# Memory projection with the weights' rest last in a step, and attention outputs split behind the attention's latest VectorE operation

## The chip, the cores and the metric

The kernel runs on one core of one Trainium2 chip. The metric is the device time of one execution in microseconds (us). Three runs of the kernel before the change gave 2080.78, 2082.31 and 2084.13 us; their median, 2082.31 us, is the time before. A separate, profiled execution gives the trace; its times are counted from the first instruction.

Engines are named as the profile names them: PE is TensorE (PEld its weight loads), DVE is VectorE, ACT is ScalarE, POOL is GpSimd, SP is SyncE.

## The reference, cut to what matters

The program is an encoder of two layers over 512 tokens of width 1024, with 256 memory tokens. Each layer is a gated feed-forward block, a self-attention mixer, a cross attention to the memory, and a second feed-forward block. The change touches the end of the mixer's stage: the projection of the memory tokens to keys and values (`m @ wkv`), and the projection of the attention's outputs (`@ w_out`).

```python
for layer in range(DEPTH):
    h = h + 0.5 * swiglu(rmsnorm(h, g), wg, wu, wd)
    if layer % 2 == 0:
        h = h + even_mixer(rmsnorm(h, mix_g), *mix_params, t5_bias, layer)
    else:
        h = h + odd_mixer(rmsnorm(h, mix_g), *mix_params)
    h = h + memory_xattn(rmsnorm(h, mg), rmsnorm(mem, sg), wq, wkv, qg, kg, wo)
    h = h + 0.5 * swiglu(rmsnorm(h, g), wg, wu, wd)

def memory_xattn(h, m, wq, wkv, qg, kg, wo):
    ...
    k, v = jnp.split(m @ wkv, 2, axis=-1)
    ...

# the end of both mixers (attention outputs o of 1024 features):
    return jnp.concatenate([out_a, out_b], axis=-1) @ w_out     # even
    return chunk_band_attention(q, k, v, rel_bias) @ w_out      # odd
```

## The kernel before, in words

**Products in three parts.** Each large operand is split into a leading part (suffix h, written by ACT in the type fp32r) and a rest (suffix l, written by DVE or POOL as the difference). A product of two such operands is three matmuls: lead by lead, lead by rest, rest by lead. Weights come through `wload` (line 166): a DMA into `wf`, then `wh` on ACT (line 161) and `wl` on DVE or, for a share of the loads, on POOL (line 163).

**Who sets the order.** PE executes its instructions in the order in which the program writes them down. The other engines' orders are made by a scheduler that simulates the program: what stands earlier in the program, or in a `high_priority` block, goes first among what is ready in that simulation. `issue_after(ins)`, used through `behind` (line 153), adds an edge of order without a semaphore: every instruction traced in its block on the engine of `ins` comes behind `ins` in that engine's queue. It does nothing to instructions on other engines.

**The weave.** In a mixer, `weave` (line 82) interleaves two generators: `gemm`, which yields an estimated cost after each piece of products, and `att`, which yields a gap. For each gap, pieces are pulled until their costs have used it up; what goes beyond is not carried over. In layer 0 a pair of heads (`attend64`, line 851) goes through these steps: queries and keys are transposed (lines 766 and 785), gap `A_QK` = 3900; the previous pair's second head is finished (transposes of the probabilities, line 837, gap `A_PT` = 1950; products with the values, line 864, gap `A_PV` = 0); the logits of head 0 (line 812), gap `A_S` = 600; the logits of head 1, gap 600; head 0 is finished (1950 and 0). In layer 1 the gaps are 4550 (`C_QK`), 2600 (`C_PT`), 600 (`C_PV`), 600 (`C_S`).

**`mark`.** `self.mark` is the latest DVE instruction that the attention has traced: the rest of the queries (line 776, the second of two), the last of four reductions of a softmax (line 825), or the last of the three rests of transposed probabilities (line 841).

**Order of the stage.** In `gemm` the six chunks of the mixer's input projection (line 706) come first, then `mem_kv` (line 1087), then `mix_out` (line 1318), which calls `out_proj` (line 635). `mem_kv` goes through 8 blocks k of the memory's width. A block has 12 matmuls of 128x512 into four PSUM banks (tag pa): for two halves i of the memory tokens and two halves c of the output, `mh` by `wh`, `mh` by `wl`, `ml` by `wh`. It yields 1300 after each i. Then the banks are copied out (lines 1110 to 1117). `out_proj` takes one attention output k after the other: at the start of a step `parts(k)` splits the output `os[k]` into `oh` (ACT, line 1327) and `ol` (DVE, line 1329) where that is not done yet, and the step's 12 matmuls (line 657) read oh, ol, oh for each of four banks, with a yield of 1300 after each second bank. The first half of the output takes k = 0 to 3, the second k = 0 to 6; what is left comes when the attention is over.

## Time and profile before

| | |
|---|---|
| median of three runs | 2082.31 us |
| the profiled execution's own time | 2083.2 us |
| its span, first to last instruction | 2081.4 us |
| granted TensorE clock, mean over the span | 0.999 |
| POOL busy | 362.0 us, 17% |
| DVE busy | 1563.2 us, 75% |
| ACT busy | 1136.0 us, 55% |
| first and last start of a matmul of `mem_kv` (line 1104) | 556.8 and 1612.8 us |
| first start of a matmul of `out_proj` that reads an `oh` | 598.4 us |

The span lies within the profiled execution's own time; 1.8 us lie around it. A row of a timeline gives the start, the duration, the engine, the line of the kernel, the operation, the tile written and the tiles read, and, in brackets, how long the engine was idle before it and who ended that. PE rows overlap, since matmuls are pipelined: the distance of two starts is what a matmul costs, not the duration in its row.

### The profile page before, as it was taken

The page shows a single profiled execution, that of the slowest core. Times are in us where ns is not written, and L with a number is a line of the kernel's source. Part 1 is how long each engine was busy: PE and PEld are TensorE (multiplying, and loading weights), DVE is VectorE, ACT ScalarE, POOL GpSimd, SP SyncE. Part 2 cuts the span into 40 slices and gives each one's busy share as a digit, 9 for nine tenths or more (in the row PEclk, how much of TensorE's full clock was granted, in tenths as well). Part 3 has the DMA queues.
Part 4 walks back from the last instruction along what each step waited for, and adds up shares of the span by engine and source line. Part 5 has one row for each costly group of instructions (what it writes and reads, how often), then busy time and mean ns, then how long its engine had stood idle before and what let it go on. Part 6 is the DMA issues. An engine that isn't in the chain of part 4 may idle for free.

```text
span 2081.4 us, 32525 instructions
## 1 busy us (share of the span) xinstructions
PE 2049.1 (98%) x12834; PEld 1826.4 (88%) x12834; DVE 1563.2 (75%) x2246; ACT 1136.0 (55%) x1701; POOL 362.0 (17%) x319
## 2 busy tenths in 40 slices
PE   8999999999999999999999999999999999999999
PEld 7989897888788889898989899988888888989897
DVE  8858687699676697685889677685668688958676
ACT  6636354556686565362556354444778566626442
POOL 1101003345431120000020000013453122000000
PEclk9999999999999999999999999999999999999999
DMA  7837535222241166574356466344224224737633
GB/s 234 208 115 196 151 95 173 88 87 81 83 136 61 61 194 171 143 190 123 107 167 180 124 178 177 100 127 148 91 81 130 94 71 144 193 120 189 166 99 94
DMA packets 86121, 279.65 MB, mean 134 GB/s; under 512 B 9680, under 2 KB 12880, under 8 KB 85968
## 3 DMA queue, kind: packets, MB, share of 16 engines
q1 hardware_dynamic: 74448, 235.62, 34.5%
q0 software_dynamic: 11520, 41.95, 11.7%
q8 instruction: 101, 1.65, 0.3%
q14 instruction: 52, 0.43, 0.1%
HBM read 271.24 MB, written 6.29 MB: 133 GB/s over the span
## 4 chain that ended last, share of the span: by engine, by line
PE 87%; DVE 7%; ACT 3%; issue 2%; DMA 1%; POOL 1%; SPq 0%; ACTq 0%; DVEq 0%; POOLq 0%
PE ps_pa L468 24%; PE ps_pa L706 11%; PE ps_pa L604 10%; PE ps_pb L468 10%; PE ps_pb L604 10%; PE ps_pa L657 4%; PE ps_pa L323 3%; PE ps_pb L812 2%; PE ps_pa L1254 1%; PE ps_pb L864 1%; PE ps_pa L1104 1%; PE ps_pb L837 1%; PE ps_pb L657 1%; PE ps_pa L1023 1%; PE ps_pb L323 1%
## 5 line engine op out<-in xcount | busy, mean ns | idle before, releaser
L161 ACT ACTIVATE wh<-wf 128x1024 fp32r<-128x1024 f32 (+2 forms) x211 | 215.4, 1022 | 334.7 <-PE ps_pa L604 114.6
L163 DVE TENSOR_TENSOR wl<-wf,wh 128x1024 fp32r<-128x1024 f32 (+2 forms) x169 | 199.5, 1184 | 32.5 <-ACT wh L161 30.5
L447 DVE TENSOR_TENSOR wl<-s,wh 128x1024 fp32r<-128x1024 f32 x108 | 132.0, 1222 | 47.3 <-ACT wh L446 47.3
L446 ACT ACTIVATE wh<-s 128x1024 fp32r<-128x1024 f32 x108 | 114.6, 1061 | 94.5 <-PE ps_pb L468 33.6
L446 ACT ACTIVATE wh<-wf 128x1024 fp32r<-128x1024 f32 x84 | 89.1, 1061 | 97.4 <-PE ps_pa L468 34.4
L525 POOL DMA_DIRECT2D s<-l_ffn_wq x40 | 35.5, 887 | 519.4 <-ACT s L524 486.4
L163 POOL TENSOR_TENSOR wl<-wf,wh 128x1024 fp32r<-128x1024 f32 x42 | 101.4, 2415 | 137.7 <-ACT wh L161 135.8
L706 PE MATMUL ps_pa<-wh,xh 128*128 128x512 f32 x384 | 122.5, 400 | 0.0
L706 PE MATMUL ps_pa<-wh,xl 128*128 128x512 f32 x384 | 119.7, 393 | 0.0
L706 PE MATMUL ps_pa<-wl,xh 128*128 128x512 f32 x384 | 119.1, 391 | 0.0
L498 POOL DMA_DIRECT2D s<-l_ffn_wq x40 | 35.6, 890 | 444.5 <-DMA s<-l_ffn_wq 150.2
L447 DVE TENSOR_TENSOR wl<-wf,wh 128x1024 fp32r<-128x1024 f32 x84 | 102.6, 1222 | 6.8 <-ACT wh L446 3.8
L614 DVE TENSOR_TENSOR dn<-ps_pa,R 128x512 f32<-128x512 f32 x48 | 33.1, 689 | 85.3 <-PE ps_pa L604 84.9
L604 PE MATMUL ps_pb<-hh,wh 128*128 128x512 f32 x352 | 95.5, 389 | 0.0
L604 PE MATMUL ps_pb<-hl,wh 128*128 128x512 f32 x352 | 95.4, 389 | 0.0
L604 PE MATMUL ps_pb<-hh,wl 128*128 128x512 f32 x352 | 95.4, 389 | 0.0
L228 POOL TENSOR_TENSOR acc<-acc,sq 128x512 f32<-128x512 f32 (+1 forms) x37 | 52.3, 1415 | 246.5 <-ACT sq L227 245.4
L604 PE MATMUL ps_pa<-hh,wh 128*128 128x512 f32 x328 | 88.9, 390 | 0.0
L604 PE MATMUL ps_pa<-hh,wl 128*128 128x512 f32 x328 | 88.6, 389 | 0.0
L604 PE MATMUL ps_pa<-hl,wh 128*128 128x512 f32 x328 | 88.6, 389 | 0.0
L614 DVE TENSOR_TENSOR dn<-ps_pb,R 128x512 f32<-128x512 f32 x48 | 33.0, 688 | 71.2 <-PE ps_pb L604 70.8
L706 PEld LDWEIGHTS ps_pa<-wh,xl 128*128 128x128 f32 x384 | 72.5, 189 | 15.9
(377 smaller groups left out, 5892.3 us busy)
## 6 DMA issues: line engine op xcount, KB each, us to landing
wf<-l_ffn_wq SPq DMA_DIRECT2D x120, 512.0 KB, 3.9
s<-l_ffn_wq SPq DMA_DIRECT2D x80, 512.0 KB, 4.9
s<-l_ffn_wq POOLq DMA_DIRECT2D x80, 512.0 KB, 6.4
wf<-l_ffn_wd SPq DMA_DIRECT2D x64, 512.0 KB, 4.2
wf<-l_w_in SPq DMA_DIRECT2D x48, 512.0 KB, 3.3
wf<-l_ffn_wd SPq DMA_DIRECT2D x32, 384.0 KB, 3.2
wf<-l_mem_wkv SPq DMA_DIRECT2D x16, 512.0 KB, 3.3
wf<-l_w_out SPq DMA_DIRECT2D x16, 512.0 KB, 3.3
```

The costliest lines, as they stand in the source:

```text
L161: self.leading = nc.scalar.activation(wh[:, sl], w[:, sl], AF.Copy)
L163: eng.tensor_sub(wl[:, sl], w[:, sl], wh.bitcast(F32)[:, sl])
L228: self.summed = (eng or nc.gpsimd).tensor_add(acc[:, :n], acc[:, :n], sq[:, :n])
L323: nc.tensor.matmul(p, w[a][:, k * P:(k + 1) * P], xs[k][c], start=k == order[0] and a == c == 0, stop=k == order[-1] and a == 1)
L446: self.leading = nc.scalar.activation(h, t, AF.Copy)
L447: self.parted = nc.vector.tensor_sub(l, t, h.bitcast(F32))
L468: self.nc.tensor.matmul(bank[:, sl], w[a][:, o:o + P], xs[k][b], start=first and z == a == b == k == 0, stop=z == a == 1 and k == KB // 2 - 1,
L604: self.nc.tensor.matmul(bank, w[a][:, j * P:(j + 1) * P], h, start=j == a == e == 0, stop=j == nb - 1 and (a, e) == ops[-1])
L614: nc.vector.tensor_mul(t, bank, f.R)
L657: nc.tensor.matmul(banks[dd], a[:, o:o + P], parts(k)[b], start=k == first and a is wh and b == 0, stop=k == last and a is wl)
L706: nc.tensor.matmul(banks[i], xs[k][a][:, i * P:(i + 1) * P], w[b][:, kk * 512:kk * 512 + 512], start=k == a == b == 0, stop=k == KB - 1 an ...
L812: nc.tensor.matmul(bank[:, o:o + n], a, b[:, :n], start=c == 0, stop=c == len(ops) - 1)
```

## The change

In `mem_kv` the matmuls of a block are regrouped: first, for each half i of the memory tokens, the four that read `wh` (`mh` by `wh` and `ml` by `wh`, two halves c), with a yield of 900 after each i; then the four that read `wl`, with a yield of 800. The number of matmuls and the sum of the yields of a block (2600) stay the same; a block is now pulled in three pieces of 4 matmuls and not in two of 6.

In `mix_out` the split of an attention output is traced in a block behind `self.mark`. Of the two instructions only the rest `ol` is on DVE, the engine of `mark`, so only it gets the edge.

```diff
@@ mem_kv
+            def products(i, ops):
+                for c in range(2):
+                    for a, b in ops:
+                        nc.tensor.matmul(banks[c][i], a[:, i * P:(i + 1) * P], b[:, c * 512:(c + 1) * 512],
+                                         start=k == 0 and a is mh and b is wh, stop=k == KB - 1 and b is wl)
+
             for i in range(2):
-                for c in range(2):
-                    for n, (a, b) in enumerate(((mh, wh), (mh, wl), (ml, wh))):
-                        nc.tensor.matmul(banks[c][i], a[:, i * P:(i + 1) * P], b[:, c * 512:(c + 1) * 512],
-                                         start=(k == 0 and n == 0), stop=(k == KB - 1 and n == 2))
-                yield 1300
+                products(i, ((mh, wh), (ml, wh)))
+                yield 900
+            for i in range(2):
+                products(i, ((mh, wl),))
+            yield 800
@@ mix_out, parts(k)
-                oh = self.xp.tile([P, S], F32R, name="oh", tag="xs", bufs=2 * KB)
-                nc.scalar.copy(oh, o)
-                ol = self.xp.tile([P, S], F32R, name="ol", tag="xs", bufs=2 * KB)
-                nc.vector.tensor_sub(ol, o, oh.bitcast(F32))
+                with self.behind(self.mark):
+                    oh = self.xp.tile([P, S], F32R, name="oh", tag="xs", bufs=2 * KB)
+                    nc.scalar.copy(oh, o)
+                    ol = self.xp.tile([P, S], F32R, name="ol", tag="xs", bufs=2 * KB)
+                    nc.vector.tensor_sub(ol, o, oh.bitcast(F32))
```

## The prediction

> **What bounds the kernel now.** The page comes first: PE is busy for almost the whole span.

> ```profile
> span 2081.4 us, 32525 instructions
> PE 2049.1 (98%) x12834; PEld 1826.4 (88%) x12834; DVE 1563.2 (75%) x2246; ACT 1136.0 (55%) x1701; POOL 362.0 (17%) x319
> ```

> So PE sets the end, and only 2081.4 - 2049.1 = 32.3 us of the span are not PE work. An edit helps by removing such idle time, or a slower clock, and harms by adding it. Next I read the waits of PE (who waited for whom: us in total, times, longest) for what the edits touch, and the four places in PE's timeline.

> ```profile
> PE ps_pb L837 <- DVE qz L776: 2.5, 2, 2.0
> PE ps_pa L1104 <- POOL wl L163: 1.9, 2, 1.0
> PE ps_pa L1104 <- DVE wl L163: 0.5, 1, 0.5
> 543.86 0.52 PE L837 MATMUL ps_pb<-ident,e 128*128 128x128 f32 x3 [2.05 <-DVE qz L776]
> 561.05 0.50 PE L1104 MATMUL ps_pa<-wl,mh 128*128 128x512 f32 x1 [1.02 <-POOL wl L163]
> 581.67 0.50 PE L1104 MATMUL ps_pa<-wl,mh 128*128 128x512 f32 x1 [0.91 <-POOL wl L163]
> 1604.78 0.50 PE L1104 MATMUL ps_pa<-wl,mh 128*128 128x512 f32 x1 [0.55 <-DVE wl L163]
> ```

> The memory's projection waits three times for a `wl`, and the transposes at 543.86 wait 2.05 us for a PSUM bank that a `qz` on DVE has to free. Why that `qz` was late stands in the timelines of DVE and POOL:

> ```profile
> 540.82 2.17 DVE L1329 TENSOR_TENSOR ol<-x,oh 128x512 fp32r<-128x512 f32 x1
> 543.02 0.69 DVE L776 TENSOR_TENSOR qz<-ps_pb,qz 64x512 fp32r<-64x512 f32 x1
> 540.07 2.37 POOL L163 TENSOR_TENSOR wl<-wf,wh 128x1024 fp32r<-128x1024 f32 x1 [1.27 <-ACT wh L161]
> L1329 DVE TENSOR_TENSOR ol<-x,oh x16: 677/690/2489, 530.4 to 1659.9; 128x512 fp32r<-128x512 f32 x16
> ```

> An attention output's rest `ol`, not needed by PE before the matmuls of line 657 much later, stood in DVE's queue ahead of the `qz`, and took 2.17 us beside a POOL split where the median of its line is 690 ns. That idle time had a second price. The stretches around it (us, then PE, PEld, DVE, ACT, POOL, and the granted clock):

> ```profile
> 541.20:544.60 3.40, 1.35 (x11) 1.10 (x10) 3.31 (x4) 2.26 (x5) 1.24 (x1) 1.00 0.30 92
> 544.60:548.00 3.40, 3.40 (x10) 2.62 (x9) 1.55 (x3) 0.29 (x1) 0.00 (x0) 0.50 0.17 67
> 548.00:551.40 3.40, 3.40 (x19) 3.00 (x19) 1.23 (x1) 1.73 (x3) 0.00 (x0) 1.00 0.00 0
> 556.00:598.00 42.00, 40.08 (x223) 32.91 (x222) 31.38 (x73) 34.15 (x73) 21.90 (x21) 1.00 0.42 138
> ```

> After a stretch in which PE worked 1.35 of 3.40 us, the granted clock was 0.50 for one stretch as long: 10 matmuls instead of 19, worth 3.40 x 0.5 = 1.7 us. The last row holds the waits of 1.02 and 0.91 us, and its clock is 1.00.

> **Part one, the memory's projection.** 8 x 12 matmuls per layer stay, and so do their DMAs, `wh` and `wl`. In a block the first reader of `wl` moves from the second place to the ninth, so `wl` has seven matmuls more, and often a step of the attention besides. The spacing of matmuls is in these rows of PE:

> ```profile
> 598.42 0.48 PE L657 MATMUL ps_pa<-oh,wh 128*128 128x512 f32 x1
> 598.74 0.39 PE L657 MATMUL ps_pa<-ol,wh 128*128 128x512 f32 x1
> 598.97 0.40 PE L657 MATMUL ps_pa<-oh,wl 128*128 128x512 f32 x1
> ```

> 0.23 us each (0.32 after another kind of work), so seven are 1.6 us, more than the longest of the three waits. All three go: 1.02 + 0.91 + 0.55 = 2.48 us. `ml` is needed one place, 0.23 us, earlier; in no row does PE wait for it, and I take nothing. The pieces are smaller: behind each logits step of a softmax come 4 matmuls, not 6, so the transposes of head 0 come 2 x 2 x 0.23 = 0.9 us sooner after their logits. The tightest place of the stage has PE's transposes at 569.15 and the end of the last exponential's sum on ACT at 567.90 + 0.19 = 568.09, a margin of 1.06 us:

> ```profile
> 569.15 1.26 PE L837 MATMUL ps_pb<-ident,e 128*128 128x128 f32 x10
> 567.90 0.19 ACT L826 ACTIVATION_READ_ACCUMULATOR e<-e,m 128x1 f32 x1
> ```

> That covers it; without that cover it would cost some tenths. All four banks of the projection now end within its last four matmuls, so their evictions come in one bunch just ahead of the first output step; this lies beside a longer wait there, below.

> **Part two, the split behind the mark.** The `ol` at 540.82 leaves its place, so the 2.05 us and the 1.7 us of half clock go: 3.75 us. With 2.48, the gains are 6.2 us.

> Against that: `parts(k)` is called at the start of step k, the mark is then the newest DVE operation of the attention, and the second matmul of the step reads `ol`. Before, `ol` could be done long ahead. Now the way from the attention's matmuls over ACT and DVE to the mark, and then `ol`, lies between PE's last attention work and this matmul, with only the pieces in between as cover. What is queued behind the waiting `ol` on DVE waits with it; what waits for it is PE, and everything behind PE.

> Where each step falls follows from the weave's costs. Layer 0: the 24 pieces of the projection start in the last gap (3000) of the diff attention and take 4; then per pair of heads gaps of 600, 600, 1950, 3900, 1950 take 1, 1, 3, 5, 3 pieces. 22 are used up when the second group's queries and keys are transposed; its gap of 3900 takes the last two (900 + 800) and two output pieces (1300 each). So k=0 starts 8 matmuls behind a `qz` mark. Then k=1 starts directly behind the transposes of a finish (gap 1950, two pieces), k=2 directly behind the logits of head 0, k=3 directly behind the next transposes, k=4 and k=5 each one piece (6 matmuls) behind transposes; k=6 and 7 come later than their mark. Layer 1, counted the same way (gaps 4550, 2600, 600, 600, 600): k=0 is 4 matmuls behind transposes, k=2 six behind a `qz`, k=4 six behind transposes; k=1, 3, 5 share their predecessor's mark and are clear.

> How late a mark is, measured from the start of the first matmul that follows its PE work, shows in the rows of PE and DVE of the trace of before. Behind transposes (typical, latest, earliest):

> ```profile
> 615.88 0.48 PE L657 MATMUL ps_pa<-oh,wh 128*128 128x512 f32 x1
> 617.79 0.55 DVE L841 TENSOR_TENSOR pz2l<-ps_pb,pz2h 128x384 fp32r<-128x384 f32 x1
> 580.28 0.48 PE L1104 MATMUL ps_pa<-wh,mh 128*128 128x512 f32 x1
> 584.42 0.55 DVE L841 TENSOR_TENSOR pz2l<-ps_pb,pz2h 128x384 fp32r<-128x384 f32 x1
> 1651.76 0.48 PE L657 MATMUL ps_pa<-oh,wh 128*128 128x512 f32 x1
> 1653.07 0.55 DVE L841 TENSOR_TENSOR pz2l<-ps_pb,pz2h 128x384 fp32r<-128x384 f32 x1
> ```

> The mark ends 618.34 - 615.88 = 2.46 us after that point, at the latest 4.69, at the earliest 1.86. I take 2.46, the middle. Behind logits, with an `ol` that already happens to follow its mark:

> ```profile
> 610.11 0.58 PE L657 MATMUL ps_pa<-oh,wh 128*128 128x512 f32 x1
> 610.53 0.40 PE L657 MATMUL ps_pa<-ol,wh 128*128 128x512 f32 x1
> 611.11 0.69 DVE L825 CUSTOM_DVE_ANT_0 e<-ps_pb,bias 128x512 f32<-128x512 f32 x1
> 611.72 0.69 DVE L1329 TENSOR_TENSOR ol<-x,oh 128x512 fp32r<-128x512 f32 x1
> ```

> The mark ends after 611.80 - 610.11 = 1.69 us, and `ol` 0.61 us behind it, at 2.30. Behind queries and keys (layer 0 twice, layer 1):

> ```profile
> 575.08 0.48 PE L1104 MATMUL ps_pa<-wh,mh 128*128 128x512 f32 x1
> 578.15 0.69 DVE L776 TENSOR_TENSOR qz<-ps_pb,qz 64x512 fp32r<-64x512 f32 x1
> 602.64 0.69 DVE L776 TENSOR_TENSOR qz<-ps_pb,qz 64x512 fp32r<-64x512 f32 x1
> 1626.33 0.48 PE L657 MATMUL ps_pa<-oh,wh 128*128 128x512 f32 x1
> 1628.84 0.69 DVE L776 TENSOR_TENSOR qz<-ps_pb,qz 64x512 fp32r<-64x512 f32 x1
> ```

> That is 3.76 and (against 598.42, quoted above) 4.91 us in layer 0, 3.20 in layer 1. The 4.91 had the projection's evictions in front of it; the new order has them behind the `qz`, so I take 3.76 and 3.20.

> The wait of PE is mark + 0.61 - cover, where the cover is 0.32 (0.42 behind logits) plus 0.23 per matmul in between. Layer 0: k=0 3.76 + 0.61 - 2.16 = 2.2; k=1 and k=3 2.46 + 0.61 - 0.32 = 2.75 each; k=2 1.9; k=4 and k=5 2.46 + 0.61 - 1.70 = 1.4 each: 12.4 us. Layer 1: k=0 2.46 + 0.61 - 1.24 = 1.8; k=2 3.20 + 0.61 - 1.70 = 2.1; k=4 1.4: 5.3 us. Together 17.7 us. With the earliest marks (1.86, 3.20) it is 13.5 us, with the latest (4.69, 4.91) 34 us; 17.7 is nearer to the low end because the latest rows had foreign DVE work ahead of the mark. An `ol` that meets a POOL split can take up to 2.49 us (the line's longest), 1.8 more than I count; the high end holds one or two of these.

> Then the clock. Four of these waits (k=0, 1, 3 of layer 0, k=2 of layer 1) are 2.05 us or longer, the length that halved the clock at 544.60, where 1.02 us at 561.05 did not. Whether a wait falls into one such stretch or is cut in two is not known, so I count two of four: 2 x 1.7 = 3.4 us.

> [...]

> Sum: -6.2 + 17.7 + 3.4 = +14.9 us on the profiled execution's 2083.2 (its span of 2081.4 and 1.8 around it): 2098.1. The median of the runs is 0.9 lower, so 2097.2 us.

> **The rivals.**
> 1. The waits come, but the clock stays up: +11.5 us, 2093.8. For it speaks that a wait cut in two by the boundary of such stretches may be as harmless as the 1.02 us were; against it that the one wait of 2.05 us did lower the clock. [...]
> 2. Faster: the marks come early enough. With the output splits gone from the stretch ahead, DVE and ACT have less queued, and if the marks then end so early that all covers suffice, only the gains stay: 2082.3 - 6.2 = 2076.1. It decides, for k=1 and k=3, at a mark that ends 0.3 us ahead of the first matmul behind the transposes; the earliest row has it 1.86 us behind, so nearly everything speaks against it, but for a step that begins elsewhere than I counted.
> 3. Only the steps directly behind their mark wait (k=1, 2, 3 of layer 0, 7.4 us) and the others are covered, without a change of the clock: 2082.3 - 6.2 + 7.4 = 2083.5.
> 4. The edge does nothing to DVE's order; the `ol` stays early, and the three `wl` waits alone go: 2082.3 - 2.5 = 2079.8.

> **How the numbers follow.** Within 0.2%, 4.2 us either way, is about what a measurement of this kernel can tell from no change. Forecast 0.47 (2097.2), rival 1 0.33 (2093.8), rival 2 0.09 (2076.1), rival 3 0.08 (2083.5), rival 4 0.03 (2079.8). Slower: 0.47 + 0.33 = 0.80; same: 0.08 + 0.03 = 0.11; faster: 0.09. The first two reach from 13.5 us of waits without a slower clock (+7.3, 2089.6) up to waits halfway between 17.7 and 34 (25.8) with three slow stretches (5.1): +24.7, 2107.0. The range goes down to 2083 to take in rival 3.

> **What would show it.** Right: PE waits in the matmuls of line 657 for `ol` of the split's line, six times between about 595 and 640 us and three times in layer 1, 1.4 to 2.8 us each; `ol` directly behind a mark in DVE's rows; no wait for `wl` in the memory's projection, none of 2 us for `qz` at 543; half clock right behind one or more of the new waits. Wrong: `ol` still ahead of 560 us, or matmuls that read it without idle time ahead of them.

## The result and the profile after

| | before | after |
|---|---|---|
| median of five runs | 2082.31 us (2080.22 to 2086.06) | 2113.43 us (2110.08 to 2117.51) |
| the profiled execution's own time | 2083.2 us | 2111.0 us |
| its span | 2081.4 us | 2109.2 us |
| granted TensorE clock | 0.999 | 0.996 |

The time after is 1.0147 times the time before (95% interval 1.0128 to 1.0167): 31.1 us slower, where 14.9 us were forecast. The sign was right and the waits that were named came, but the size was twice the forecast and lies above the range, and one of the two parts was taken for a gain and is a cost. The trace read below is of the second fastest of the five executions, so only 27.8 of the 31.1 us are in it; the mean granted clock of the other four was 0.992 to 0.995.

The page of after:

```profile
PE 2059.1 (98%) x12830; PEld 1829.8 (87%) x12834; DVE 1562.0 (74%) x2246; ACT 1136.6 (54%) x1701; POOL 361.9 (17%) x319
```

DVE, ACT and POOL do what they did. PE's busy time is 10 us longer with the same matmuls, part of which is a slower clock, below; the rest of the 27.8 us is waiting. The waits of PE in after (in total, times, longest), first for 340 to 740 us (layer 0), below the dots for 1400 to 1760 us (layer 1):

```profile
PE ps_pa L657 <- DVE ol L1336: 9.7, 6, 2.4
PE ps_pb L937 <- POOL orr L248: 2.4, 1, 2.4
PE ps_pa L657 <- ACT qk L1116: 1.4, 1, 1.4
PE ps_pa L657 <- DVE x L670: 1.2, 1, 1.2
...
PE ps_pa L657 <- ACT qk L1116: 2.8, 1, 2.8
PE ps_pa L657 <- DVE ol L1336: 2.8, 2, 2.1
PE ps_pa L1104 <- ACT qk L731: 1.4, 1, 1.4
PE ps_pb L812 <- DVE x L869: 1.0, 1, 1.0
```

The three waits for `wl` in the memory's projection are gone, and so is the 2.0 us wait for `qz`. In their place stand the forecast waits for `ol`, 9.7 + 2.8 = 12.5 us, and some that were not forecast: for the copies of the projection's banks (L1116), for `orr`, for `x`, for `qk` of L731. The `ol` waits one by one, in PE's timeline of after:

```profile
600.37 0.80 PE L657 MATMUL ps_pa<-ol,wh 128*128 128x512 f32 x1 [2.01 <-DVE ol L1336]
608.20 0.50 PE L657 MATMUL ps_pa<-ol,wh 128*128 128x512 f32 x1 [2.39 <-DVE ol L1336]
616.84 0.79 PE L657 MATMUL ps_pa<-ol,wh 128*128 128x512 f32 x1 [1.77 <-DVE ol L1336]
626.39 0.50 PE L657 MATMUL ps_pa<-ol,wh 128*128 128x512 f32 x1 [2.04 <-DVE ol L1336]
653.98 0.50 PE L657 MATMUL ps_pa<-ol,wh 128*128 128x512 f32 x1 [0.66 <-DVE ol L1336]
660.27 0.50 PE L657 MATMUL ps_pa<-ol,wh 128*128 128x512 f32 x1 [0.87 <-DVE ol L1336]
1651.42 0.50 PE L657 MATMUL ps_pa<-ol,wh 128*128 128x512 f32 x1 [2.12 <-DVE ol L1336]
1677.77 0.50 PE L657 MATMUL ps_pa<-ol,wh 128*128 128x512 f32 x1 [0.66 <-DVE ol L1336]
```

The wait ahead of 608.20 in PE's and DVE's timelines of after: the first matmul of the step, the mark (the last rest of transposed probabilities), then `ol` directly behind it, and 1.10 us after its start the second matmul runs.

```profile
605.32 0.48 PE L657 MATMUL ps_pa<-oh,wh 128*128 128x512 f32 x1
606.64 0.55 DVE L841 TENSOR_TENSOR pz2l<-ps_pb,pz2h 128x384 fp32r<-128x384 f32 x1
607.10 1.04 DVE L1336 TENSOR_TENSOR ol<-x,oh 128x512 fp32r<-128x512 f32 x1
```

Then the clock. In the traces of before and after the granted clock changes only at points a multiple of 3.41 us apart; these are the stretches of that grid around the longer waits of after (us, then PE, PEld, DVE, ACT, POOL, the granted clock, and the DMA's columns):

```profile
596.40:599.80 3.40, 0.52 (x2) 0.19 (x1) 1.97 (x3) 3.35 (x6) 2.35 (x1) 1.00 0.16 66
599.80:603.20 3.40, 2.83 (x7) 2.26 (x8) 3.30 (x5) 3.34 (x6) 0.00 (x0) 0.50 0.46 154
606.60:610.00 3.40, 1.80 (x8) 1.52 (x9) 1.54 (x3) 0.21 (x1) 0.99 (x1) 1.00 0.00 0
613.50:616.90 3.40, 1.57 (x6) 0.64 (x6) 3.25 (x11) 2.72 (x9) 0.00 (x0) 0.99 0.43 154
616.90:620.30 3.40, 3.40 (x11) 2.82 (x12) 0.18 (x1) 0.13 (x2) 0.54 (x2) 0.50 0.23 77
623.70:627.10 3.40, 1.36 (x8) 0.96 (x7) 2.22 (x4) 1.66 (x4) 0.35 (x2) 1.00 0.20 67
627.10:630.50 3.40, 3.40 (x10) 2.64 (x9) 0.00 (x0) 0.00 (x0) 0.00 (x0) 0.50 0.00 0
1634.00:1637.40 3.40, 1.30 (x8) 0.78 (x6) 2.01 (x4) 3.38 (x8) 0.72 (x4) 1.00 0.37 111
1637.40:1640.80 3.40, 2.68 (x6) 1.80 (x7) 3.16 (x6) 3.40 (x8) 0.37 (x1) 0.51 0.44 154
1640.80:1644.20 3.40, 3.40 (x10) 2.63 (x9) 1.76 (x5) 0.98 (x2) 1.69 (x2) 0.50 0.00 0
```

Five stretches run at half clock, where before had one. In them PE is busy 2.83 + 3.40 + 3.40 + 2.68 + 3.40 = 15.7 us, of which half, 7.9 us, is the price by this estimate; before paid 1.7 us. Each of their runs begins behind a stretch in which PE worked 0.52 to 1.57 us. The longest `ol` wait, 2.39 us, is cut in two by the grid: its stretch 606.60:610.00 still has 1.80 us of work, and nothing follows.

### The profile page after: what moved, and what is told of

It reads as the page before. It is cut to its first block, busy times and chain, and to the rows that moved or that the text cites. A ratio compares the mean times of both kernels' runs of the same rounds, so it can differ in the third digit from the quotient of the medians.

```text
span 2109.2 us, 32502 instructions
## 1 busy us (share of the span) xinstructions
PE 2059.1 (98%) x12830; PEld 1829.8 (87%) x12834; DVE 1562.0 (74%) x2246; ACT 1136.6 (54%) x1701; POOL 361.9 (17%) x319
## 4 chain that ended last, share of the span: by engine, by line
PE 62%; DVE 5%; ACT 2%; DMA 1%; issue 1%; POOL 0%; DVEq 0%; ACTq 0%; SPq 0%
PE ps_pa L468 18%; PE ps_pa L604 8%; PE ps_pb L604 7%; PE ps_pb L468 7%; PE ps_pa L706 6%; PE ps_pa L657 4%; PE ps_pa L1260 1%; PE ps_pb L864 1%; PE ps_pa L323 1%; PE ps_pb L812 1%; PE ps_pb L657 1%; PE ps_pa L1104 1%; PE ps_pb L837 1%; DVE xl L211 1%; DVE wl L163 1%
## 5 line engine op out<-in xcount | busy, mean ns | idle before, releaser
L161 ACT ACTIVATE wh<-wf 128x1024 fp32r<-128x1024 f32 (+2 forms) x211 | 215.3, 1022 | 343.3 <-PE ps_pa L604 112.4
L163 DVE TENSOR_TENSOR wl<-wf,wh 128x1024 fp32r<-128x1024 f32 (+2 forms) x169 | 199.4, 1183 | 34.9 <-ACT wh L161 32.6
L163 POOL TENSOR_TENSOR wl<-wf,wh 128x1024 fp32r<-128x1024 f32 x42 | 101.4, 2415 | 150.8 <-ACT wh L161 140.9
L706 PE MATMUL ps_pa<-wh,xh 128*128 128x512 f32 x384 | 121.9, 399 | 0.1
L706 PE MATMUL ps_pa<-wh,xl 128*128 128x512 f32 x384 | 118.9, 391 | 0.0
L706 PE MATMUL ps_pa<-wl,xh 128*128 128x512 f32 x384 | 118.6, 390 | 0.0
L826 ACT ACTIVATE e<-e,m 128x128 f32<-128x128 f32 (+3 forms) x128 | 70.8, 554 | 40.0 <-DVE m L825 39.9
```

Of the source, the lines that this page charges most:

```text
L161: self.leading = nc.scalar.activation(wh[:, sl], w[:, sl], AF.Copy)
L163: eng.tensor_sub(wl[:, sl], w[:, sl], wh.bitcast(F32)[:, sl])
L706: nc.tensor.matmul(banks[i], xs[k][a][:, i * P:(i + 1) * P], w[b][:, kk * 512:kk * 512 + 512], start=k == a == b == 0, stop=k == KB - 1 an ...
L826: nc.scalar.activation(e, e, AF.Exp, bias=m[:, i:i + 1], scale=-1.0, accum_out=rs[:, i:i + 1])
```

## The experiments

Each kernel was timed in rounds against the kernel before on the same chip: 2079.12 us for the first four, 2080.06 us for the next four, 2079.26 us for the last two. Differences below are of these medians, with the interval of the ratio in brackets. The theory on record was that the `ol` placed behind a late mark makes PE wait (part two), and that part one costs nothing; the rival was that part one, or something the prediction did not list, has a price of its own.

### Each part alone, and the split with more distance

**The regrouping alone (e1).** The first hunk of the diff, the splits as before:

```diff
@@ mem_kv
+                products(i, ((mh, wh), (ml, wh)))
+                yield 900
...
+                products(i, ((mh, wl),))
+            yield 800
```

> Only the memory projection's regrouping; the attention outputs are split as before. Theory A (the late splits are what costs): the three waits for wl (2.5 us) go and nothing comes, so about 2.5 us less than before, 2080. Theory B (the regrouping costs by itself: the evictions of its four banks come in one bunch, and the scale of the diff attention is waited for behind a shorter piece of work): the waits of the changed kernel's trace that do not name ol come here too, 1.4 and 2.8 us for the evicted banks and 2.4 us for POOL's orr, and with 2.5 us gained and perhaps a slow stretch of the clock it is 4 to 8 us slower than before, 2086 to 2090. The 2.05 us wait near 543 us and the half clock behind it stay in both.

Measured: 2092.36 us, +13.2 (1.0042 to 1.0077): theory B's waits came, at more than its 4 to 8 us, and with a stretch at half clock from 1627.60 on (1627.60:1631.00, clock 0.50). The waits of PE in this kernel, layer 0 and, below the dots, layer 1:

```profile
PE ps_pb L937 <- POOL orr L248: 2.4, 1, 2.4
PE ps_pa L657 <- ACT qk L1116: 2.3, 2, 1.5
PE ps_pa L657 <- DVE x L670: 1.2, 1, 1.2
...
PE ps_pa L657 <- ACT qk L1116: 3.1, 1, 3.1
PE ps_pa L1104 <- ACT qk L731: 1.4, 1, 1.4
PE ps_pb L812 <- DVE x L869: 1.0, 1, 1.0
```

So the waits of after that nobody forecast belong to part one. The longest of them, in PE's timeline of this kernel, with the exponential and the copy on ACT that it waits for:

```profile
1623.94 1.17 PE L1104 MATMUL ps_pa<-wl,mh 128*128 128x512 f32 x4
1628.17 0.79 PE L657 MATMUL ps_pa<-oh,wh 128*128 128x512 f32 x1 [3.06 <-ACT qk L1116]
...
1626.81 0.74 ACT L826 ACTIVATE e<-e,m 128x512 f32<-128x512 f32 x1
1627.53 0.59 ACT L1116 COPY qk<-ps_pa 128x512 f32<-128x512 f32 x1
```

The projection's last four products end at 1625.1 and the first product of the output follows them on PE with nothing between; it needs a bank that the copy frees, and the copy stands on ACT behind the exponentials of the softmax. In before, by the rows of ACT and PE, the first copy was made 4.6 us ahead of the first output product, and between this product and the projection's last one lay logits of the attention:

```profile
1609.69 0.57 ACT L1110 COPY qk<-ps_pa 128x512 f32<-128x512 f32 x1
1612.76 0.39 PE L1104 MATMUL ps_pa<-wh,ml 128*128 128x512 f32 x1
1612.99 0.28 PE L812 MATMUL ps_pb<-kz0h,qz 128*128 128x256 f32 x1
1614.29 0.40 PE L657 MATMUL ps_pa<-oh,wh 128*128 128x512 f32 x1
...
560.95 1.01 POOL L248 TENSOR_TENSOR orr<-ov,mhalf 128x4 f32<-128x4 f32 x1
562.31 0.60 PE L937 MATMUL ps_pb<-ident,orr 128*128 128x128 f32 x4
```

The last two rows are the `orr` of before: it ended at 561.96, 0.35 us ahead of its reader, and this reader stood late itself, since PE had just waited 1.02 us for `wl`. That wait had covered the lateness of `orr`; with the new order PE comes to the transposes without it, two products sooner, and waits 2.4 us. Some 1 us of these 2.4 has another source: `orr` itself took 2.06 us, where it took 1.01 before. In POOL's and DVE's timelines of after a `wl` split on DVE begins within 0.02 us of it:

```profile
557.44 2.06 POOL L248 TENSOR_TENSOR orr<-ov,mhalf 128x4 f32<-128x4 f32 x1
557.42 1.21 DVE L163 TENSOR_TENSOR wl<-wf,wh 128x1024 fp32r<-128x1024 f32 x1
```

In the kernels below `orr` takes 2.06 us with a wait of 1.9 in e5, and 1.01 us with a wait of 0.9 in e6. What made `orr` longer was not tested.

**The edge alone (e2).** The second hunk, the products in the old order and pieces:

```diff
@@ mix_out, parts(k)
+                with self.behind(self.mark):
```

> Only the split behind the mark; the memory's projection has its old order. Theory A: the 3.75 us of the qz wait and its slow stretch go; but the steps now begin at the old places of the weave, k=0 of layer 0 directly behind a qz mark, k=4 and k=5 directly behind transposes, and in layer 1 k=0 behind logits, k=1 behind transposes, k=3 and k=5 six matmuls behind a mark: some 13 us of waits for ol in layer 0 and 8 in layer 1 by the prediction's lengths (9 and 6 at the lengths that the changed kernel showed, about 0.8 of those). With 3 to 5 slow stretches of 1.7 us it is 16 to 24 us slower than before, 2098 to 2106. Theory B: the two parts share the 31 us, and this one alone gives clearly less than 16 us.

Measured: 2100.58 us, +21.5 (1.0081 to 1.0126). Its waits of PE, layer 0 and layer 1:

```profile
PE ps_pa L657 <- DVE ol L1330: 12.3, 5, 5.3
PE ps_pa L1104 <- POOL wl L163: 1.9, 2, 1.0
...
PE ps_pa L657 <- DVE ol L1330: 6.9, 4, 2.1
```

The mechanism of part two stands alone: 19.2 us of waits for `ol`, and four stretches at half clock (two in 598.00:604.80, then 656.00:659.40 and 1628.80:1632.20, clock 0.50), within theory A's 16 to 24 us. The `wl` waits stay, as they must with the old order. The longest `ol` wait, 5.3 us, is the first step's: its first product starts at 594.61, and its mark, a `qz` behind the copies of the projection's banks on DVE, ends at 599.50, 4.89 us later. That is the latest mark of the prediction (4.91).

**The split behind a mark, but early (e3, e4).** The outputs that are there are split behind the mark already at blocks 4 and 6 of the projection, so products lie between split and use. The later outputs are split as in the change. e3 has the old order of products, e4 the whole change; `ahead` calls `parts(k)` for every output that is there:

```diff
@@ mem_kv
+            if k in (4, 6):
+                self.ahead()
```

> As the split-behind-the-mark alone, but every output that is there is split, behind the mark of that moment, when the memory's projection begins its blocks 4 and 6, and again at each later step for those that came since: the edge stays, and there are at least two blocks (some 5 us of PE work) between a mark and the first use. Theory A (what costs is that the use follows the mark at once): no wait for ol is left in steps 0 to 3, the qz wait near 543 us is gone too, so up to 3.75 us faster than before, 2078 to 2080; at most 1 to 3 us of waits for outputs 4 to 7. Theory C (being behind the attention's operations costs as such, wherever it is traced): waits for ol stay and it is over 10 us slower than before.

> The changed kernel with the outputs split earlier: at blocks 4 and 6 of the memory's projection, behind the mark of that moment, and at each later step for those that came since. Theory A (late splits are the cost): the waits for ol (12.5 us) and the slow stretches behind them go, and both gains stay: 2076 to 2078. Theory B (the regrouping costs by itself): the waits for the evicted banks (1.4 and 2.8 us, or more, as no wait for ol hides them now) and for orr (2.4 us) stay: 2081 to 2088.

Measured: 2085.32 us, +6.2 (1.0021 to 1.0040), with the old order; 2095.19 us, +16.1 (1.0054 to 1.0088), with the whole change. With distance the edge loses most of its price (21.5 to 6.2), but e3 is slower than before, where theory A had it up to 3.75 us faster. In layer 0 the rests of the first five outputs are done by 587.8, ahead of the first product that reads one (596.46), and none of them is waited for. One wait that is left is seen in PE's timeline of e3, at a step that still comes directly behind its mark, with products at about half their speed after it (from 644.59 to 647.15 the starts lie 0.43 us apart, from 637.73 to 638.41 0.23):

```profile
643.66 0.51 PE L657 MATMUL ps_pa<-ol,wh 128*128 128x512 f32 x1 [2.26 <-DVE ol L1332]
```

The other waits of e3 that before does not have are 1.6 us for an `x` of L869 and 0.7 us for an `ol` in layer 1. With the whole change 16.1 us stay, more than theory B's 2 to 9 and close to the 13.2 of the regrouping alone: splitting early repairs most of part two, and not part one.

### What in the regrouping costs: the order or the pieces

Part one changes two things: the order of the products in a block, and that a block is pulled in three pieces of 4 and not in two of 6.

The next three kernels keep the splits as before and hand out a block's 12 products, in the one order or the other, through one loop (`ops()` lists them, `n` counts them):

```diff
@@ mem_kv
+            for i, c, a, b in ops():
...
+                nc.tensor.matmul(banks[c][i], a[:, i * P:(i + 1) * P], b[:, c * 512:(c + 1) * 512],
...
+                if n in (6, 12):
+                    yield 1300
```

e5 has the change's order in these halves; e6 the same, but the last block k = 7 in the old order; e8 the old order with `n in (4, 8, 12)` and yields of 900, 900 and 800.

> The memory projection's matmuls in the regrouped order, but pulled in two pieces of 6 matmuls with yields of 1300, as before, so that the attention's operations keep their places among them; outputs split as before. Theory P (the pieces of 4 are what the regrouping costs: less PE work behind each step of the attention): the waits for orr (2.4 us), for x of line 670 (1.2), the longer transposes and value products (2 us in layer 0) are gone, the wl waits too, and the time is within 3 us of before. Theory Q (the bunched evictions of the four banks are what it costs): PE's waits for the copies of line 1110 stay, 1.4 to 3 us in each layer, a slow stretch with the longer of them, and the time is 3 to 7 us above before.

Measured: 2084.39 us, +4.3 (1.0010 to 1.0028). The size is in theory Q's range, but its sign is missing: no wait for the copies of the projection's banks is listed in either layer. PE waits 1.9 us for `orr`, and several times 0.4 to 1.4 us for others.

> As the regrouped order in pieces of 6, but the last block of the eight in the old order, so that the banks end one half of the memory tokens after the other, as before; outputs split as before. Theory Q: the waits for the banks' copies go, and this kernel is 3 to 7 us faster than the one with all blocks regrouped. Theory P: no difference between the two. By both it should then be level with before or up to 2.5 us faster (the three wl waits), unless orr, which was hidden behind the first wl wait, is waited for instead (1 us).

Measured: 2083.56 us, +3.5 (1.0004 to 1.0022). The 0.8 us between these two is less than their intervals, and the lists differ by 1.0 us at `orr`, so nothing here shows a price of the banks ending together in the last block.

> The memory projection's matmuls in their old order, but pulled in three pieces of 4 with yields of 900, 900 and 800, as in the changed kernel; outputs split as before. Theory P: most of the 13 us that the regrouping alone costs come here too, at least 6 us, with PE's waits for orr, for the transposes and for x of line 670. Theory Q: the banks end staggered, and the time is within 3 us of before.

Measured: 2091.64 us, +11.6 (1.0034 to 1.0067). Pieces of 4 in the old order cost nearly what the whole regrouping costs (13.2), the new order in pieces of 6 a third of it. Together that is 15.9, so the two are not a plain sum. The two waits of the pieces in layer 1, in PE's timeline of that kernel:

```profile
1622.36 0.50 PE L657 MATMUL ps_pa<-oh,wh 128*128 128x512 f32 x1 [1.18 <-ACT qk L1118]
1625.24 0.80 PE L657 MATMUL ps_pa<-oh,wh 128*128 128x512 f32 x1 [1.91 <-DVE vp L1125]
```

These are again waits for the projection's banks, copied too late, here in the old order. With less work pulled into the short gaps the projection's last product starts 214.0 us behind the first product of the mixer's input projection (1405.36 to 1619.4) and not 209.0 (1403.83 to 1612.8 in before), and so meets another place of the attention.

**Both parts, with pieces of 6 (e10).** e5's loop and the edge; the lines taken out are those of the changed kernel:

```diff
@@ mem_kv
-                products(i, ((mh, wh), (ml, wh)))
-                yield 900
...
+                if n in (6, 12):
+                    yield 1300
```

> Both parts of the change, but the regrouped products are handed out in two halves of six as before's are, not in pieces of 4. Theory that the costs add: the edge alone (21.5) and the order alone in halves (4.3) give 25.8 above before, about 2106 us beside 2080, and the rest to the whole change, some 5 us, is the pieces'. Rival that the pieces' cost lies beside the waits for ol: as the whole change, 31 above before, about 2111. Rival that the order in halves lies beside them too: as the edge alone, 2101.5.

Measured: 2108.65 us, +29.4 (1.0127 to 1.0154). The whole change in pieces of 4 has 31.1 (1.0128 to 1.0167): with the edge in place the pieces no longer matter within the intervals. The rival that the pieces' cost lies beside the waits for `ol` holds. The other rival, that the order in halves lies beside them too, falls: against the edge alone (21.5) e10 has 7.9 us more. Its waits in layer 0 and layer 1 show the exchange:

```profile
PE ps_pa L657 <- DVE ol L1338: 12.8, 5, 5.9
...
PE ps_pa L657 <- DVE ol L1338: 7.7, 4, 2.7
```

Here PE waits 20.5 us for `ol`, and no wait for the banks' copies is listed; after waits 12.5 us for `ol` and 1.4 + 2.8 for the copies. By these sums the waits for the banks just ahead of a step let the mark catch up, and the waits for `ol` shrank, from 20.5 to 12.5 us.

### Is there a version that is faster than before

**Outputs 0, 1 and 2 split behind the mark at blocks 1, 3 and 5 (e7)**, the other splits without an edge, on top of e6:

```diff
@@ mem_kv
+            if k in {1: 0, 3: 1, 5: 2}:
+                self.ahead({1: 0, 3: 1, 5: 2}[k])
```

> As the regrouped order in pieces of 6 with the last block old, and the outputs 0, 1 and 2 split behind the mark one at a time at the start of the memory projection's blocks 1, 3 and 5; outputs 3 to 7 are split as before, without an edge. Theory A (an edge to the mark costs only where the use follows at once): no wait for ol, the qz wait of 2 us near 543 us and its slow stretch of 1.7 us are gone, so 3 to 4 us faster than the kernel without the edge and 4 to 6 us faster than before, 2073 to 2075. Against it: the three splits crowd the attention's DVE work in the projection's stage, and what is gained at 543 us is given back there: level with the kernel without the edge.

Measured: 2082.59 us, +2.5 (1.0007 to 1.0026), against +3.5 for e6. The 0.9 us between the two medians is within their intervals, and the 2073 to 2075 of theory A was missed. In the trace there is no wait for `ol` and only 0.4 us for `qz` in layer 0 (2.7 in e6), but 1.9 us for `x` of L869 (0.7 in e6), so 1.2 of the 2.3 us gained there were given back by the next wait in line. This trace is of the slowest of its ten executions (2087.66 us), with a mean granted clock of 0.998, where the traced execution of e6 has 1.000.

**Only the split that stood in the way put behind the mark (e9).** Before's order and pieces, no edge at an output step; only the third output of layer 0 gets its split behind the mark, at the first block of the projection. In the trace of e9 the splits of the first two outputs come with it: three stand in DVE's queue from 543.21 on, directly behind the attention's latest rest, where before has them at 530.41, 532.65 and 540.82.

```diff
@@ mem_kv
+            if k == 0 and pre == "l0_":
+                self.ahead(2)
```

> Only the split of layer 0's third attention output is put behind the latest operation of the attention, at the start of the first product step of memory's projection; everything else is as before, the order of its products too. Theory: before loses 2.05 us of PE at the wait for qz behind that split, and 1.7 us by the half clock that follows it; with the split moved to where VectorE is idle both go and nothing takes their place: 3.75 us less, about 2076.3 us beside 2080. Rival: the half clock comes by the wait that is late next (the weight's rest, or orr), or the split is late for a product at its new place: level with before, within 2 us.

Measured: 2076.28 us against 2079.26, -3.0 (0.9982 to 1.0000), where -3.75 was expected. The stretches of this kernel where before had its `qz` wait and its half clock:

```profile
541.20:544.60 3.40, 3.40 (x17) 2.83 (x16) 3.37 (x7) 3.21 (x6) 0.00 (x0) 1.00 0.48 159
544.60:548.00 3.40, 3.40 (x19) 2.98 (x19) 1.64 (x2) 2.10 (x4) 0.00 (x0) 1.00 0.20 54
```

PE is busy in both, and the clock is 1.00 in both; no `ol` wait comes in exchange. It is the only kernel here whose median lies below before's, by 0.14%. The ratio from all its runs is 0.9991, about 1.9 us, and its interval touches 1: a gain that the traces explain and the timing barely resolves. The traces show it in its place: from the first product of L706 to the first of L323 behind the cross attention, layer 0 takes 347.53 us in before (380.15 to 727.68) and 343.72 us in e9 (378.98 to 722.70), 3.81 less, and layer 1 takes 334.10 and 334.12.

## Why the prediction was right and wrong

**Right: the gains.** The `ol` at 540.82 left its place, and the 2.05 us and the 1.7 us of half clock behind it went. e9 leaves this gain alone: 3.8 us in its trace, 3.0 us between the medians, with an interval that touches no gain. The 1.7 us need not be paid in every execution, since in the rows of e6, below, a `qz` wait as long has no half clock behind it.

**Right: the waits for `ol`, a little too large.** For layer 0 the prediction had 2.2, 2.75, 1.9, 2.75, 1.4, 1.4; the rows show 2.01, 2.39, 1.77, 2.04, 0.66, 0.87. For layer 1 it had 1.8, 2.1, 1.4; the rows show 2.12 and 0.66, and none for the first step, where the wait for the copies had come before. Sum 12.5 instead of 17.7. The rule used, mark plus split minus the products in between, carries, and so did the covers that were counted. What was too large is the mark behind transposes: in after it ends 1.87, 2.33, 1.86, 2.09 and 1.86 us behind the first matmul, near the earliest row of before (1.86) and not the 2.46 that was taken. The profile also counts a wait from the modelled end of the matmul ahead, which makes it 0.1 to 0.2 us shorter than the prediction's measure, from start to start. Two of the six come at 654 and 660 us, not by 640. e2, e3 and e7 show the cause: the edge alone costs 21.5 us, with distance 6.2, and in e7, where every split with an edge has distance, no `ol` is waited for.

**Wrong: the step "Part one", costed as a pure gain of 2.48 us.** Beside the edge alone (21.5) it adds 9.6 us to the change; that is 12.1 of the 16.2 us by which the forecast missed. Two steps of it failed. For the smaller pieces it looked at the tightest place, "a margin of 1.06 us", and held that this covers it: one margin at one place was tested, but smaller pieces move every place of the attention against the projection. And "their evictions come in one bunch just ahead of the first output step; this lies beside a longer wait there": in layer 1 the eviction is itself the longest wait, 2.8 us, and the `ol` wait that should have hidden it is gone. By itself part one costs 13.2 us (e1), most of it by the pieces (e8, 11.6), some by the order (e5, 4.3). Beside the edge it is the other way round: the order adds 7.9 us (e10 against e2), and the pieces 1.7 more, which is within the intervals. That the banks end together is neither needed nor enough for the late copies: e8 waits for them without it, and e5 has it and does not wait. The three `wl` waits did go, but what one of them had covered came out: `orr`, 2.4 us for a removed wait of 1.0, of which some 1 us is the longer `orr`.

**Wrong in size: the clock.** Two slow stretches were counted, 3.4 us; there are five, 7.9 us. One place, 1634 to 1637, has nothing to do with `ol`: it is the copies' wait of part one, and it is two stretches long. The other three stand behind waits for `ol`, the first of them together with the wait for a copy.

**How the 31 us come about.** Of the 27.8 us in the trace of after 27.1 lie in the two stages that the change touches, from the first product of L706 to the first of L323 behind the cross attention: 16.5 in layer 0 and 10.6 in layer 1. In the profiled execution the waits for `ol` (12.5), the copies (1.4 + 2.8), `orr` (2.4), `x` of L670 (1.2), 0.7 more for L731 (0.7 in before) and 1.0 for L869 add 22.0; the waits gone are 2.5 for `wl` and some 2.1 for `qz`; the clock adds 7.9 - 1.7 = 6.2. That makes 23.6 of the 27.8 us of the span. The page bears it out: PE's time outside its work rose from 32.3 to 2109.2 - 2059.1 = 50.1 us, 17.8, where the waits make 22.0 - 4.6 = 17.4; and its busy time rose by 10.0 us, of which the clock has 6.2. The rest, some 4 us, is in matmuls and not in waits. About half of it is the edges of the waits: the matmul ahead of one counts as busy for 0.48 us where the next could start 0.32 us behind it, and the matmul behind one takes 0.33 us to the next start and not 0.23 (608.20 to 608.53). That is 0.26 us a wait, by an estimate 2.3 us for the 13 waits that came less the 4 that went. Where the other half lies no experiment separated. The two parts alone add to 13.2 + 21.5 = 34.7, so some 3.6 us of their costs lie beside each other, no more than the intervals allow.

**The rivals.** Rival 1, that the clock stays up, fell. Rival 2, that the marks come early enough, fell with the rows of `ol`. Rival 3, that only the steps directly behind their mark wait, is nearest where the later waits shrank to 0.66 and 0.87, but even these did not vanish. Rival 4, that the edge does nothing to DVE's order, fell with the rows of `ol` directly behind their marks, and with e2.

Not settled is which of the attention's places each of the pieces' 11.6 us comes from. The waits in e8 for the copies, for `x` and for `vp` are seen, and that a different cut of the same 96 products moves them; why the old cut meets better places was not tried.

## What to carry to other kernels

A split or copy put "behind the latest operation" makes its reader wait unless enough of the reader's own work lies between that operation and the reader (here +21.5 us with the edge at the use, +6.2 with distance): count the products, and give the order edge to an operation several pieces ahead of its use, not at its use. Where two streams are woven by costs, the size of the pieces is part of the schedule (here +11.6 us for pieces of 4): a change of grain moves every meeting point, so cost it by a run of the grain alone and not by one margin. And before a small wait is removed, look at what becomes late next behind it, since a wait can be the cover of another, as here the 1.02 us for `wl` were for `orr`, then waited for 2.4 us.

## What the runs showed of the hardware

```profile
543.50:546.90 3.40, 1.56 (x9) 1.37 (x10) 3.31 (x5) 1.74 (x4) 0.42 (x1) 1.00 0.45 154
546.90:550.30 3.40, 3.40 (x20) 2.98 (x19) 1.68 (x3) 1.06 (x1) 0.00 (x0) 1.00 0.02 5
```

So in these rows 1.80 us of idle time in a stretch left the full clock, 1.83 did not, and 1.84 is seen without half clock behind it; a sharper limit they do not show. Here the same 2 us wait cost 2 us or nearly 4 by where it lay: 2.39 us at 608.20 was harmless, 2.04 us at 626.39 had 627.10:630.50 at 0.50 behind it. This is read from the traces; no kernel shifted a wait on the grid on purpose.

**A slow stretch can last without a new wait.** In after the stretch at 1640.80 stays at half clock (0.50, with 3.40 us of work) behind one, 1637.40, that had 2.68 us of work, while the clock came back behind 599.80 with 2.83 us. The other slow stretches inside the spans of before and after, each with 3.40 us of work, had full clock behind them. So in after a stretch at half clock with 2.68 us of work had half clock behind it, where one at full clock with 1.60 us (1647.7 to 1651.1) had full clock. In matmuls 2.68 us need not be more than 1.60, since at half clock one took about twice as long (10 and 19 in a stretch of before, in the prediction's rows; 6 and 7 in these two of after).
